# Score products with k's low part and the sample's value products on 128 rows instead of 64, in a two-layer attention and FFN trunk

## The chip, the cores and the metric

One Trainium2 chip, one of its cores. The metric is the device time of one execution in microseconds (us), median of the runs shown. Engines: PE is TensorE (matrix products; PEld its weight loads), DVE is VectorE, ACT ScalarE, POOL GpSimd, SP issues most DMAs.

## What is computed

Two layers of a streaming encoder, for a prompt of 512 tokens and a sample of 64 new tokens behind a cache of 128, with the same weights. Cut to what matters here:

```python
p = xn @ w_in                      # q k v of three branches A, B, C (8, 8, 4x2 heads of 64), gate logits
# A: band attention with a bias by distance; prompt and sample
logits = einsum('bqhd,bkhd->bhqk', q, keys) * 64**-0.5 + bias
o_a = einsum('bhqk,bkhd->bqhd', softmax(logits), vals)
# B: stick-breaking: weights from log_sigmoid(z) and reversed sums over keys of log_sigmoid(-z)
# C: two softmax maps per head, p0 - lam * p1, times v (128 wide), normalised per head
x = x + (sum_n sigmoid(gate_n) * (o_n @ w_branch[n])) @ w_out
x = x + (gelu(causal_conv3(xn @ w_gate)) * (xn @ w_up)) @ w_down
```

All in float32.

## The kernel before

**Tokens and weights.** The 64 sample tokens and the 512 prompt tokens stand side by side as 576 columns, worked in two halves of 288. The weights come in chunks of 512 KB. Each product of the main stream is split: a value is written as a high part (fp32r) and a low part (the rest), and hi\*hi, hi\*lo and lo\*hi are summed in PSUM. So a chunk of eight 128-row blocks is 48 products of 288 columns, named `mv..`, `mk..`, `mq..`, `mg..`, `mb..`, `mo`, `mu..`, `md` (the digit in a name is the layer, the last letter the branch, f the FFN; `mm` at L129 to L131 makes them all).

**Attention units.** A unit is 128 columns of q, k and v, that is two heads of 64. There are four units to a branch and layer, 24 in all. `prep_k` (L605) makes from k the tile KD: for head e, rows 64e to 64e+63 hold k's high part, and the other 64 rows a copy of k itself. `prep_q` (L634) makes X: q's high part on the same rows as k's high part, q's low part on the others. So one product of 128 rows gives hi\*hi + lo\*k. What is left, q's high part with k's low part, needs 64 rows: `prep_k` writes k's low part to KL on rows 64e to 64e+63, and `scores` (L656) and `zmm` in `head_b` (L881) issue behind each KD product a KL product over these 64 rows, into the same PSUM columns. The widths are 512, 384, 256 and 128 columns for a head (a causal triangle of tiles), so there are 4 KL products to a head.

**The sample.** Its attention weights come to `sw`: 128 cache keys in columns 0 to 127, the 64 new keys in columns 128 to 255 on 64 rows. `sample_pv` (L804) makes two products, cache values `cv` on 128 rows and new values `natsv` on 64 rows, in float32, for which the profile shows two records each.

**What sets the order.** Every engine works its own queue in order. The order is written out at build time: the main stream issues its products, and after each the generators of the attention steps are asked (`tick`, L141) whether their next step is due by an estimate of the engines' clocks. The estimate of a product (L130) goes by its columns alone, not by its rows. Steps therefore stand between main products in fixed places, and an engine waits at its queue's head where a result is late.

**Buffers that the change touches.** KL (one buffer), `sw` (one), `natsv` (two, alternating), and `ch`, high parts of B's running sums (two buffers of their own). `bias` is a pair of 128x512 buffers, used in branches A and C only.

Of the kernel before, what the change touches and what calls it, by code (L numbers as in the profile page):

```python
# [16 lines left out]
P = 128  # L17
D = 1024
ND = 8
S = 512  # L20
# [13 lines left out]
# column blocks of P kept as keys by queries: (key tile -> offset in the 1280 wide layout)  # L34
SEG = {0: 0, 1: 512, 3: 896, 2: 1024}
# row blocks of P kept as queries by keys: (query tile -> offset in the 1280 wide layout)
# [9 lines left out]
def trunk_kernel(ctx: ExitStack, tc: tile.TileContext, a: dict, o: dict):  # L46
# [26 lines left out]
    # The order of issue follows an estimate of the engines' clocks: a generator's next step is  # L73
    # issued when what it depends on should be there, so that no engine waits at its queue's head.
    clk = {"PE": 0.0, "ACT": 0.0, "DVE": 0.0, "POOL": 0.0}
    cx = {"t": 0.0, "eng": None, "last": 0.0}
    gens = []  # [label, generator, time from which the next step may be issued]
# [100 lines left out]
    def bank(kind, nm, hold):  # L178
        """a PSUM bank, as soon as one is free in emission order; hold collects it for give()"""
        yield from until(lambda: free[kind] and min(free[kind]) <= clk["PE"])  # L180
        take(kind, nm, hold)
# [22 lines left out]
    # parameter rows -> per-partition columns  # L204
# [49 lines left out]
    stc = const.tile([P, 4, NF], F32, name="stc")  # L254
    identb = const.tile([P, P], BF16, name="identb")
# [5 lines left out]
    # every vector on 128 rows, so that a row pitch shorter by one reads shifted windows  # L261
# [22 lines left out]
    def bias_band(l, aid, tab, queue=nc.gpsimd):  # L284
        """bias by distance, one row per head: the reversed table of the band"""
        h = []
        yield from bank("z", f"ep{l}", h)
        ep = h[0][1]
        mm(ep[0:8, 0:P], tab[:, 1, :], aid, True, True)
        mm(ep[0:8, P:2 * P], tab[:, 0, :], aid, True, True)  # L290
        ev = slot(f"ev{l}")
        vector.memset(ev[0:8, 0:319], 0.0)
        vector.memset(ev[0:8, 575:576], 0.0)
        vector.tensor_copy(ev[0:8, 319:575], ep[0:8, 0:256])
        give(h)
        vector.tensor_scalar(ev[0:8, 0:319], ev[0:8, 0:319], ev[0:8, 319:320], None, op0=ALU.add)
        queue.dma_start(ebias[l * 8:l * 8 + 8, :], ev[0:8, 0:EW])

    def bias_buckets(t5t, oh):
        """the same of the shared buckets"""  # L300
        ev = slot("ev5")
        for c0, cn in ((0, 512), (512, 64)):
            h = []
            yield from bank("z", f"ep5{c0}", h)
            ep = h[0][1]
            mm(ep[0:4, 0:cn], t5t, oh[0:32, c0:c0 + cn], True, True)
            vector.tensor_copy(ev[0:4, c0:c0 + cn], ep[0:4, 0:cn])
            give(h)
        nc.gpsimd.dma_start(ebias[16:20, :], ev[0:4, 0:EW])

    def setup(aid, tabs, t5t, oh):
        """constants of the later steps, between the first chunks"""
# [10 lines left out]
        for l in range(DEPTH):  # L323
            nb = const.tile([P, 24], F32, name=f"nbg{l}")
            vector.tensor_scalar(nb, par[l, 0][:, 16:40], -1.0, None, op0=ALU.mult)
            par[l, 2] = nb
            lam_init = 0.8 - 0.6 * math.exp(-0.3 * l)
            ls = const.tile([P, 2], F32, name=f"ls{l}")
            lt = sm.tile([P, 64], F32, tag="lt", name=f"lt{l}", bufs=1)
            for j in range(2):  # L330
                vector.tensor_tensor_reduce(out=lt, in0=lp[:, l, 2 * j, :], in1=lp[:, l, 2 * j + 1, :], scale=1.0,
                                            scalar=0.0, op0=ALU.mult, op1=ALU.add, accum_out=ls[:, j:j + 1])
            yield
            scalar.activation(ls, ls, AF.Exp)
            yield
            nl = const.tile([P, 1], F32, name=f"nlam{l}")
            # -(e0 - e1 + init) = (e1 - init) - e0
            vector.scalar_tensor_tensor(nl, in0=ls[:, 1:2], scalar=-lam_init, in1=ls[:, 0:1],
                                        op0=ALU.add, op1=ALU.subtract)
            lamc[l] = nl  # L340
            sc = const.tile([P, 1], F32, name=f"sub{l}")
            vector.tensor_scalar(sc, par[l, 0][:, 40:41], 1.0 - lam_init, None, op0=ALU.mult)
            subc[l] = sc
# [12 lines left out]
    chunks = []  # L356

    def chunk(nm, src, kt, act, evac, ncol=1, pre=None, pre_ev=None, post=None, norm=None, half=None, twin=None):
        """half: only one half of the tokens; twin: the earlier chunk whose weights serve again"""
# [15 lines left out]
    def split(i):  # L375
        """the weights' high and low parts, half a chunk at a time"""
# [91 lines left out]
    # Newton's step for r = rsqrt(v) from a = K rsqrt(v), K^3 = 1/2:  r = (3 K^2 - v a^2) a  # L468
    KR = 0.5 ** (1.0 / 3.0)

    def rstd_steps(ps, n, r, t):
        """r = rsqrt(mean + eps) of a PSUM region; exp/ln with a Newton step; t scratch"""
# [24 lines left out]
    def norm_tile(nm, d, x, g):  # L497
        """x * g split for the products, squares summed"""
# [46 lines left out]
    def load_bias(row, nm):  # L545
        """[queries, 512 keys], right aligned; the last 64 keys are hidden from the first 64 queries"""
# [13 lines left out]
    def natural(u, src, off, kind):  # L560
        """[cols, tokens] -> token rows: the k / v outputs, and v for P V"""
# [15 lines left out]
        nats = sm.tile([T, P], F32, tag="nats" + kind, name=f"nats{kind}{nm}", bufs=2 if kind == "v" else 1)  # L577
# [8 lines left out]
    def prep_v(u):  # L586
# [4 lines left out]
        u["vns"] = u["nats"]  # L591
# [14 lines left out]
    def prep_k(u):  # L606
# [4 lines left out]
        KL = ap_.tile([P, S], F32R, tag="KL", name=f"KL{nm}", bufs=1)  # L611
        u["KD"], u["KL"] = KD, KL
# [7 lines left out]
        for e in range(2):  # L620
# [8 lines left out]
            vector.tensor_tensor(KL[r, :], kp[r, :], KD[r, e, :].bitcast(F32), op=ALU.subtract)  # L629
# [26 lines left out]
    def scores(u, e, qt, z, c0):  # L656
        n = (qt + 1) * P
        r = slice(64 * e, 64 * e + 64)
# [3 lines left out]
        mm(out, u["X"][r, e, qs], u["KL"][r, 0:n], False, True)  # L662
        return out

    def soft(u, e, A, st, b, qts, nm, after):
        """exp(logits - max) of some query tiles, laid out by query, and 1 / sum"""
# [21 lines left out]
    def to_keys(A, nm, ph, pl, grp, flag):  # L688
        """[q, keys] -> [keys, q], hi and lo"""
# [22 lines left out]
    def pv_head(u, e, ph, pl, dst, nm):  # L712
        """dst[64e:64e+64, T:] = (P V)^T of head e"""
# [60 lines left out]
    def sample_soft(u, nm, b):  # L774
# [24 lines left out]
        w = sm.tile([P, 256], F32, tag="sw", name=f"sw{nm}", bufs=1)  # L799
# [6 lines left out]
    def sample_pv(u, w, nm, h):  # L806
# [4 lines left out]
        mm(ps[:, 0:P], u["vns"], w[0:64, P:2 * P], False, True)  # L811
# [16 lines left out]
    def softplus_to(dst, z):  # L828
        """dst = max(z, 0) + ln(1 + exp(-|z|))"""
# [7 lines left out]
    def sample_b(u):  # L837
# [4 lines left out]
        # both heads side by side, keys of the cache | new keys (rows past 64 masked)  # L842
# [10 lines left out]
        w = sm.tile([P, 256], F32, tag="sw", name=f"sw{nm}", bufs=1)  # L853
# [6 lines left out]
    def head_b(u, e):  # L860
        l, br, p, nm0 = u["id"]
        nm = f"{nm0}{e}"
        X, KD, KL = u["X"], u["KD"], u["KL"]
        r = slice(64 * e, 64 * e + 64)
        A = wide("a", f"A{nm}")
        sh, sl = wide("ph", f"sh{nm}", F32R), wide("pl", f"sl{nm}", F32R)
        ch = ap_.tile([P, 384], F32R, tag="ch", name=f"ch{nm}", bufs=2)
# [4 lines left out]
        def zmm(z, kt, c0, start):  # L872
# [4 lines left out]
            mm(out, KL[r, ks], X[r, e, kt * P:512], False, False)  # L877
# [8 lines left out]
        def keep(sg, z, flag):  # L886
            """softplus of z, in two parts"""
# [5 lines left out]
        def weights(sg, z, hold, flag, eng):  # L893
            """exp of the finished exponents, in two parts"""
# [22 lines left out]
        # sums over later key tiles, kept by query: kt 2 += kt 3  # L917
# [5 lines left out]
        # kt 1 += kt 2  # L923
# [18 lines left out]
        for t_, c_ in ((sh, ch), (sl, cl)):  # L942
            mm(z0, negt, t_[:, g0], False, False)
            mm(z0[:, P:512], negones, c_, False, t_ is sl)
        yield
# [5 lines left out]
    def head_c(u):  # L951
# [48 lines left out]
        # headwise norm over the 128 values (partitions)  # L1000
# [37 lines left out]
    def spawn_attention(u):  # L1038
# [7 lines left out]
        else:  # L1046
            u["left"], u["qk"] = 3, 9 if br == 0 else 3
# [8 lines left out]
    def unit(l, br, p, prev, prev2, first):  # L1056
# [5 lines left out]
        # while slots are free, v and q needn't share one place  # L1062
# [27 lines left out]
        def pre_q():  # L1090
# [6 lines left out]
            elif br == 2:  # L1097
                u["bias"] = [load_bias(16 + p, nm)]
# [14 lines left out]
    def sigmoid_steps(g, l, br, c):  # L1113
        # sigmoid(y) = exp(-ln(1 + exp(-y)))
# [43 lines left out]
    def layer(l):  # L1158
# [38 lines left out]
        # w_out and the residual  # L1197
# [22 lines left out]
        # FFN  # L1220
# [94 lines left out]
        def down_final(fs):  # L1315
            """one half of the tokens after the other, so that the first half's rows leave meanwhile"""
# [41 lines left out]
        # the states of the last f are there before the last group of w_down starts  # L1358
# [11 lines left out]
    fin = {"n": [0, 0], "ys": []}  # L1370
    # rows of each half: first column, rows, where they go
# [30 lines left out]
    def final_rstd(h, rp):  # L1402
        """1 / rms of the rows of a half, one column pair per block of rows"""
# [46 lines left out]
    def final_second():  # L1450
        """rows of the second half as their tiles get ready; they stay in PSUM"""
# [35 lines left out]
    def load_x(i):  # L1487
        """all prompt rows of a quarter of the columns"""
# [31 lines left out]
    # the first three chunks grow with the rows of x as they get turned  # L1520
# [46 lines left out]
    def split_first(i):  # L1567
        """chunks 0 and 1 in slots, as three are held at a time"""
# [101 lines left out]
def _constants():  # L1670
# [3 lines left out]
    # keys (rows) by queries (columns): masked where key >= query; sample: two heads of 64 queries  # L1674
# [31 lines left out]
```

## Time and profile before

| | |
|---|---|
| median of three runs | 2258.51 us (2256.84 to 2266.4) |
| profiled execution, first to last instruction | 2255.2 us |
| PE busy | 2230.0 us (99%), 15911 products |
| DVE / ACT / POOL busy | 1395.3 (62%) / 1044.5 (46%) / 397.2 (18%) us |
| DMA | 200.5 MB, mean 89 GB/s |
| mean granted TensorE clock | 0.988 of full speed |

How to read it: the span is divided nearly wholly among products on PE, so what counts is how far each product's start lies from the next one's. A product's own "busy" time includes its way through the array and overlaps the next; the distance of starts doesn't. Two forms appear in a row: `128*128 128x288` says rows\*columns of the weights that stand in the array, then rows x columns of what is streamed through it. The trunk's attention lies at about 45 to 640 us (layer 0) and 1155 to 1700 us (layer 1), the FFN behind each.

### The profile page before, as it was taken

Reading aid. Unit: us, or ns where it says so; the run is one execution under the profiler, and the core shown is the slowest. Engines: PE = TensorE matmul, PEld = TensorE weight load, DVE = VectorE, ACT = ScalarE, POOL = GpSimd, SP = SyncE. Lnnn points to the kernel's source line nnn. Section 1 sums busy time; section 2 is a strip of 40 time slices with the busy share of each in tenths; the row PEclk is TensorE's granted clock in tenths of the full one; section 3 lists DMA queues with packets and bytes.
Section 4 is the critical chain, followed back from the end, with each engine's and each line's share of the span. In section 5 each row is a group of like instructions: output and inputs, shape, how many; then the busy total and the mean of one; then the engine's idle time right before and its main releaser. Section 6 shows DMA issues by size and latency. Waiting matters only on the chain.

```text
span 2255.2 us, 39749 instructions
## 1 busy us (share of the span) xinstructions
PE 2230.0 (99%) x15911; PEld 2136.7 (95%) x15911; DVE 1395.3 (62%) x2852; ACT 1044.5 (46%) x2057; POOL 397.2 (18%) x520
## 2 busy tenths in 40 slices
PE   8999999999999999999999999999999999999998
PEld 7989999999999999999998999999999999999998
DVE  7786655666556656556567656566674666556564
ACT  5557666544534323223345477665445343223334
POOL 2012121111032212112110111211110222112121
PEclk9999999999999999999999999999999999999999
DMA  7342222222232222222242322222222423222222
GB/s 212 96 137 75 84 73 77 76 87 74 80 123 75 85 85 85 84 83 79 92 134 72 101 58 78 74 76 85 76 88 80 126 66 95 84 85 85 75 85 72
DMA packets 326563, 200.50 MB, mean 89 GB/s; under 512 B 10544, under 2 KB 320754, under 8 KB 326314
## 3 DMA queue, kind: packets, MB, share of 16 engines
q1 hardware_dynamic: 324618, 194.88, 29.0%
q0 software_dynamic: 1760, 3.08, 0.4%
q8 instruction: 125, 2.05, 0.4%
q14 instruction: 60, 0.49, 0.1%
HBM read 176.54 MB, written 25.83 MB: 90 GB/s over the span
## 4 chain that ended last, share of the span: by engine, by line
PE 93%; DVE 4%; issue 1%; ACT 1%; POOL 1%; DMA 0%; SPq 0%; DVEq 0%; POOLq 0%; ACTq 0%
PE md L131 11%; PE mg1f L131 6%; PE mg0f L131 6%; PE mu1f L131 6%; PE mu0f L131 6%; PE mo L131 4%; PE mg0b L131 3%; PE mg1b L131 2%; PE mg1a L131 2%; PE mg0a L131 2%; PE mg0c L131 2%; PE mg1c L131 2%; PE mv1a L131 1%; PE mv1b L131 1%; PE mk1a L131 1%; PE mb0a L131 1%
## 5 line engine op out<-in xcount | busy, mean ns | idle before, releaser
L102 DVE TENSOR_TENSOR x<-md,x 128x288 f32<-128x288 f32 x192 | 86.7, 454 | 117.1 <-PE md L131 116.3
L102 ACT CAST whid<-wrd 128x512 fp32r<-128x512 f32 (+1 forms) x88 | 46.8, 579 | 138.0 <-PE md L131 87.9
L131 PE MATMUL md<-hh0f,whid 128*128 128x288 f32 x352 | 104.9, 298 | 3.5 <-DVE x L102 3.5
L131 PE MATMUL mu0f<-xhf,wlou0f 128*128 128x288 f32 x352 | 103.8, 295 | 0.0
L131 PE MATMUL mu1f<-xhf,wlou1f 128*128 128x288 f32 x352 | 103.8, 295 | 0.0
L131 PE MATMUL md<-hh0f,wlod 128*128 128x288 f32 x352 | 103.8, 295 | 0.0
L131 PE MATMUL mg0f<-xhf,whig0f 128*128 128x288 f32 x352 | 103.8, 295 | 0.0
L131 PE MATMUL mg1f<-xhf,whig1f 128*128 128x288 f32 x352 | 103.8, 295 | 0.0
L131 PE MATMUL mg0f<-xhf,wlog0f 128*128 128x288 f32 x352 | 103.7, 295 | 0.0
L131 PE MATMUL mg1f<-xhf,wlog1f 128*128 128x288 f32 x352 | 103.7, 295 | 0.0
L131 PE MATMUL mu0f<-xlf,whiu0f 128*128 128x288 f32 x352 | 103.7, 295 | 0.0
L131 PE MATMUL mu1f<-xlf,whiu1f 128*128 128x288 f32 x352 | 103.7, 295 | 0.0
L131 PE MATMUL md<-hl0f,whid 128*128 128x288 f32 x352 | 103.6, 294 | 0.0
L131 PE MATMUL mg0f<-xlf,whig0f 128*128 128x288 f32 x352 | 103.6, 294 | 0.0
L131 PE MATMUL mg1f<-xlf,whig1f 128*128 128x288 f32 x352 | 103.6, 294 | 0.0
L131 PE MATMUL mu0f<-xhf,whiu0f 128*128 128x288 f32 x352 | 103.6, 294 | 0.0
L131 PE MATMUL mu1f<-xhf,whiu1f 128*128 128x288 f32 x352 | 103.6, 294 | 0.0
L131 PE MATMUL md<-hh1f,whid 128*128 128x288 f32 x288 | 85.7, 297 | 2.7 <-DVE x L102 2.7
L131 PE MATMUL md<-hh1f,wlod 128*128 128x288 f32 x288 | 84.9, 295 | 0.0
L131 PE MATMUL md<-hl1f,whid 128*128 128x288 f32 x288 | 84.8, 294 | 0.0
L131 PE MATMUL mo<-ml,whio 128*128 128x288 f32 x256 | 75.6, 295 | 0.8 <-DVE ml L102 0.8
L131 PE MATMUL mo<-mh,wloo 128*128 128x288 f32 x256 | 75.5, 295 | 0.0
(957 smaller groups left out, 8519.4 us busy)
## 6 DMA issues: line engine op xcount, KB each, us to landing
wrd<-in_w_down SPq DMA_DIRECT2D x40, 512.0 KB
wrg0f<-in_w_up SPq DMA_DIRECT2D x22, 512.0 KB
wru0f<-in_w_up SPq DMA_DIRECT2D x22, 512.0 KB
wrg1f<-in_w_up SPq DMA_DIRECT2D x22, 512.0 KB
wru1f<-in_w_up SPq DMA_DIRECT2D x22, 512.0 KB
wro<-in_w_out SPq DMA_DIRECT2D x16, 512.0 KB
xspill<-x SPq DMA_DIRECT2D x16, 288.0 KB
x<-xspill SPq DMA_DIRECT2D x16, 288.0 KB
```

Source lines behind the costliest of these rows:

```text
L102: return f(*args, **kw)
L131: nc.tensor.matmul(out, lhsT=lhsT, rhs=rhs, start=start, stop=stop, skip_group_check=True)
```

## The change

KL becomes one constant tile with a plane for each head. Its other 64 rows are set to zero once at the start, `prep_k` writes k's low part on the 64 rows as before, and the KL products run over all 128 rows of X and KL: the zero rows add nothing. `sw` and the two `natsv` buffers become constant tiles too; their rows 64 to 127 are zero from the start (in branch B, `sw` is written whole each time by an exponential of masked values), and the second sample product runs over 128 rows. To make room, B's `ch` tiles take the `bias` buffers, idle in B, and the q chunk of the first two C units waits in the written order until the last B unit's `ch` products are issued.

```diff
+    KL = const.tile([P, 2, S], F32R, name="KL")
+    natsv = [const.tile([P, P], F32, name=f"natsv{i}") for i in range(2)]
+    sw = const.tile([P, 2 * P], F32, name="sw")
+    for i in range(4):
+        cs = slice(i * P, (i + 1) * P)
+        vector.tensor_scalar(KL[64:128, 0, cs], onesd[64:128, :], 0.0, None, op0=ALU.mult)
+        vector.tensor_scalar(KL[0:64, 1, cs], onesd[0:64, :], 0.0, None, op0=ALU.mult)
+    for t in (*natsv, sw[:, P:2 * P]):
+        gpsimd.memset(t[64:128, :], 0.0)
 ...
-            vector.tensor_tensor(KL[r, :], kp[r, :], KD[r, e, :].bitcast(F32), op=ALU.subtract)
+            vector.tensor_tensor(KL[r, e, :], kp[r, :], KD[r, e, :].bitcast(F32), op=ALU.subtract)
 ...
-        mm(out, u["X"][r, e, qs], u["KL"][r, 0:n], False, True)
+        mm(out, u["X"][:, e, qs], KL[:, e, 0:n], False, True)
 ...
-        mm(ps[:, 0:P], u["vns"], w[0:64, P:2 * P], False, True)
+        mm(ps[:, 0:P], u["vns"], w[:, P:2 * P], False, True)
 ...
-        ch = ap_.tile([P, 384], F32R, tag="ch", name=f"ch{nm}", bufs=2)
+        ch = ap_.tile([P, 512], F32R, tag="bias", name=f"ch{nm}", bufs=2)[:, 0:384]
 ...
-            mm(out, KL[r, ks], X[r, e, kt * P:512], False, False)
+            mm(out, KL[:, e, ks], X[:, e, kt * P:512], False, False)
 ...
+                drain_while(lambda: prev is not None and prev.get("ch", 2 if prev["id"][1] == 1 else 0) > 0, "ch")
```

On PE, ACT and SP the built instructions stand in the same order before and after, one for one. DVE and POOL get instructions at the start alone. DVE's queue before, from its first instruction of the kernel (`ones`, `epsc` are constants, `g` the gains of the first norm, `xst` the sample's rows):

```order
L102 MEMSET onesd 128x128
L102 TENSOR_SCALAR ones_88<-onesd 128x128
L102 MEMSET epsc 128x1 x2
L102 COPY g_152<-g_150 128x8
L102 COPY xst<-xts 128x512
```

and now:

```order
L102 MEMSET onesd 128x128
L102 TENSOR_SCALAR ones_88<-onesd 128x128
L102 MEMSET epsc 128x1 x2
L102 TENSOR_SCALAR KL<-onesd 64x128 x8
L102 COPY g_167<-g_165 128x8
L102 COPY xst<-xts 128x512
```

Eight instructions that write KL's zeros stand ahead of the copy of `g`; POOL gets three memsets of 64x128 ahead of its first DMA. At run time a few instructions wait for more than before: the first `ch` cast of each layer for old bias loads, and the first bias load and memset of a C unit for the `ch` products of the last B unit.

## Rows read from the trace of the kernel before

**Rows 1.** The page: busy time by engine; the chain that ended last.

```profile
PE 2230.0 (99%) x15911; PEld 2136.7 (95%) x15911; DVE 1395.3 (62%) x2852; ACT 1044.5 (46%) x2057; POOL 397.2 (18%) x520
...
PE 93%; DVE 4%; issue 1%; ACT 1%; POOL 1%; DMA 0%; SPq 0%; DVEq 0%; POOLq 0%; ACTq 0%
```

**Rows 2.** Waits of PE, 45 to 1690 us: total us, times, longest us.

```profile
PE md L131 <- DVE x L102: 3.5, 9, 0.7
```

**Rows 3.** Timeline, PE and PEld: start, duration, engine, line, operation, form [idle before].

```profile
46.02 0.19 PEld L131 LDWEIGHTS mk0a<-xhm,whik0a 128*128 128x128 f32 x1
46.15 0.29 PE L131 MATMUL mk0a<-xhm,whik0a 128*128 128x288 f32 x1
...
49.96 0.18 PEld L131 LDWEIGHTS s0a<-KL0a,X0a 64*128 64x128 f32 x1 [0.19 <-issue]
49.96 0.44 PE L131 MATMUL s0a<-KL0a,X0a 64*128 64x384 f32 x1
```

**Rows 4.** Timeline of PE: scores of the first C unit, twelve products up to 395.30.

```profile
391.07 0.40 PE L131 MATMUL s0c<-KD0c,X0c 128*128 128x512 f32 x1
391.40 0.50 PE L131 MATMUL s0c<-KL0c,X0c 64*128 64x512 f32 x1
...
395.30 0.40 PE L131 MATMUL mb0a<-oh0a,whib0a 128*128 128x288 f32 x1
```

**Rows 5.** Timeline of PE: products on 128 rows without a KL product near.

```profile
358.60 0.28 PE L131 MATMUL zb0b<-ch0b,tri 128*128 128x256 f32 x1
358.72 0.34 PE L131 MATMUL zb0b<-sl0b,tri 128*128 128x384 f32 x1
...
369.50 0.40 PE L131 MATMUL zc0b<-sh0b,tri 128*128 128x512 f32 x1
369.73 0.33 PE L131 MATMUL zc0b<-ch0b,tri 128*128 128x384 f32 x1
369.91 0.39 PE L131 MATMUL zc0b<-sl0b,tri 128*128 128x512 f32 x1
...
376.50 0.22 PE L131 MATMUL o0b<-sh0b,VS0b 128*128 128x128 f32 x1
376.56 0.22 PE L131 MATMUL o0b<-sl0b,VS0b 128*64 128x128 f32 x1
```

**Rows 6.** Timeline of PE: scores of a B head, nine products up to 1296.10.

```profile
1294.25 0.22 PE L131 MATMUL za1b<-X1b,KD1b 128*128 128x128 f32 x1
...
1294.65 0.23 PE L131 MATMUL za1b<-mbs,identb 128*128 128x128 bf16 x1
1294.69 0.36 PE L131 MATMUL za1b<-X1b,KD1b 128*128 128x256 f32 x1
...
1296.10 0.31 PE L131 MATMUL za1b<-X1b,KD1b 128*128 128x128 f32 x1
```

**Rows 7.** KL's products in layer 0's branch A: count, duration ns min/median/max, first and last start.

```profile
L131 PE MATMUL s0a<-KL0a,X0a x32: 322/439/686, 49.2 to 154.3; 64*128 64x512 f32 x8, 64*128 64x384 f32 x8, 64*128 64x256 f32 x8, 64*128 64x128 f32 x8
```

**Rows 8.** Timeline of PE: the sample's value products of one unit.

```profile
1239.75 0.48 PE L131 MATMUL spv1a<-sw1a,natsv1a 64*128 64x128 f32 x2
1240.17 0.40 PE L131 MATMUL mk1a<-xhm,whik1a 128*128 128x288 f32 x1
```

**Rows 9.** The ten stretches at half clock ahead of 2250 us, by engine: their sum.

```profile
sum 51.20, PE 51.20 PEld 46.91 DVE 34.01 ACT 31.10 POOL 3.22; mean PE 5.12 PEld 4.69 DVE 3.40 ACT 3.11 POOL 0.32
```

**Rows 10.** Timeline of PE inside one of these stretches.

```profile
1232.20 0.44 PE L131 MATMUL mv1a<-xhm,whiv1a 128*128 128x288 f32 x1
1232.44 0.44 PE L131 MATMUL mv1a<-xlm,whiv1a 128*128 128x288 f32 x1
```

**Rows 11.** Branch A of layer 0: us, busy time of PE, PEld, DVE, ACT, POOL; clock.

```profile
45.00:175.00 130.00, 130.00 (x833) 114.25 (x833) 101.22 (x292) 68.31 (x164) 16.82 (x32) 0.95 0.39 112
```

**Rows 12.** Timeline of DVE at the start; issue of the first C bias on SP's queue.

```profile
3.12 0.17 DVE L102 COPY g<-g 128x8 f32<-128x8 f32 x1 [1.85 <-PE g L135]
...
375.39 0.53 SPq L548 DMA_DIRECT2D bias0c<-ebias  x1
```

More of the change, by code (lines that the diff above doesn't have):

```diff
@@ L576, in natural @@
         yield
-        nats = sm.tile([T, P], F32, tag="nats" + kind, name=f"nats{kind}{nm}", bufs=2 if kind == "v" else 1)
+        if kind == "v":
+            nats = natsv[(br * 4 + p) % 2][0:T, :]
+        else:
+            nats = sm.tile([T, P], F32, tag="natsk", name=f"natsk{nm}", bufs=1)
         vector.tensor_copy(nats, tp2[0:T, 0:P])
@@ L590, in prep_v @@
         yield from natural(u, u["vf"], 0, "v")
-        u["vns"] = u["nats"]
+        u["vns"] = natsv[(br * 4 + p) % 2]
         vn = u["nat"]
@@ L610, in prep_k @@
         KD = ap_.tile([P, 2, S], F32R, tag="KD", name=f"KD{nm}", bufs=1)
-        KL = ap_.tile([P, S], F32R, tag="KL", name=f"KL{nm}", bufs=1)
-        u["KD"], u["KL"] = KD, KL
+        u["KD"] = KD
         h = []
@@ L657, in scores @@
         n = (qt + 1) * P
-        r = slice(64 * e, 64 * e + 64)
         qs = slice(qt * P, qt * P + P)
@@ L798, in sample_soft @@
         yield
-        w = sm.tile([P, 256], F32, tag="sw", name=f"sw{nm}", bufs=1)
+        w = sw
         vector.tensor_copy(w[:, 0:P], tp[:, 0:P])
@@ L852, in sample_b @@
         yield
-        w = sm.tile([P, 256], F32, tag="sw", name=f"sw{nm}", bufs=1)
+        w = sw
         scalar.activation(w, z[:, 0:256], AF.Exp)
@@ L862, in head_b @@
         nm = f"{nm0}{e}"
-        X, KD, KL = u["X"], u["KD"], u["KL"]
-        r = slice(64 * e, 64 * e + 64)
+        X, KD = u["X"], u["KD"]
         A = wide("a", f"A{nm}")
         sh, sl = wide("ph", f"sh{nm}", F32R), wide("pl", f"sl{nm}", F32R)
-        ch = ap_.tile([P, 384], F32R, tag="ch", name=f"ch{nm}", bufs=2)
+        ch = ap_.tile([P, 512], F32R, tag="bias", name=f"ch{nm}", bufs=2)[:, 0:384]
         cl = ap_.tile([P, 384], F32R, tag="cl", name=f"cl{nm}", bufs=2)
@@ L944, in head_b @@
             mm(z0[:, P:512], negones, c_, False, t_ is sl)
+        u["ch"] -= 1
         yield
@@ L1046, in spawn_attention @@
         else:
-            u["left"], u["qk"] = 3, 9 if br == 0 else 3
+            u["left"], u["qk"], u["ch"] = 3, 9 if br == 0 else 3, 2 if br == 1 else 0
             spawn(lab, (head_a if br == 0 else head_b)(u, 0))
```

## Prediction

> **What bounds the kernel now.** The page comes first: PE is busy 99% of the span and makes up 93% of the chain that ended last [rows 1]. The waits of PE say the same from the other side: over the whole stretch that holds attention, its largest wait for another engine adds up to 3.5 us [rows 2]. So what shortens PE's own sequence shortens the kernel, until another engine becomes late. Busy time doesn't tell whether PE's time is well spent, so the next view is the timeline, and there the distance from one start to the next. A main product of 288 columns takes 0.13 us, and its weights are loaded while the product ahead of it still runs: the load at 46.02 is 0.13 us ahead of its product [rows 3]. At a KL product this isn't so. Load and product start together at 49.96, and the load follows 0.19 us in which PEld stood idle [rows 3]. The idle time is put down to nothing else that the profile shows ("issue"). A load takes about 0.18 us [rows 3], so a product whose load isn't hidden should cost that much more, and the KD product behind it the same on the way back.
>
> **What a pair costs now, and what on 128 rows.** The first C unit's score run has six pairs (KD and KL of 512, 512, 384, 384, 256 and 128 columns); from 391.07 to 395.30 they take 4.23 us [rows 4]. The price of products that stay on 128 rows: 0.23 us at 512 columns, 0.18 at 384, 0.12 at 256, 0.06 at 128 [rows 5]. These rows also hold accumulation into one PSUM region and new weights at every product, as the pairs have them, and one product on 64 columns of weights, which follows at 0.06 us like the rest: fewer columns cost nothing, so what costs at KL is rows. The six pairs at these prices are 2 x (2 x 0.23 + 2 x 0.18 + 0.12 + 0.06) = 2.00 us. The run gives back 4.23 - 2.00 = 2.23 us, or 0.37 a pair. Both ways at 0.19 would be 0.38, so the two readings agree. A B head has three pairs and three masks in 1296.10 - 1294.25 = 1.85 us, a mask taking 0.04 [rows 6]. At full price that is 2 x (0.06 + 0.12 + 0.18) + 0.12 = 0.84 us, so 1.01 / 3 = 0.34 a pair. Each branch has 32 KL products in a layer, as the row of A's shows [rows 7], so A and C have 128 in the two layers and B 64: 128 x 0.37 + 64 x 0.34 = **69 us**.
>
> **The sample.** The trace before has no float32 value product of new keys on 128 rows. Its two records on 64 rows take 1240.17 - 1239.75 = 0.42 us [rows 8]. The nearest rows bound the gain: nothing, if the doubled work of float32 is what costs, and 0.4 if it pays entry, middle and exit. I take 0.3, near the pair's 0.37, since it too leaves 128 rows and returns. 24 units make 24 x 0.3 = **7 us** (bounds 0 to 10).
>
> **The clock.** The granted clock stands at half (1.2 instead of 2.4 GHz) in ten stretches ahead of the last microseconds, 51.2 us in all [rows 9]. Ahead of every one of the ten PE had been in a run of score pairs; it never fell in the FFN, which is denser. At half clock a main product takes 0.24 us [rows 10] instead of 0.13 [rows 3]. So these stretches hold 51.2 x (1 - 0.13 / 0.24) = 23 us that full clock would give back. The pairs above were priced in runs at full clock, so nothing is counted twice. If runs of half the length leave PE without its gaps, the falls should go. But in branch A a new wait may stand right behind a run (below), so I take two thirds, **16 us** (bounds 0 and 23).
>
> **What becomes late.** PE's and DVE's queues keep their order, and PE now reaches the steps that read DVE's results sooner. In branch A of layer 0 DVE works 101 of 130 us [rows 11]. PE would give up 32 x 0.37 + 4 x 0.3 = 13 us there, and half of what its lower clock (0.95) costs, some 3 us: 114 us, of which DVE fills 89%. Two in-order queues that wait for each other in turn don't run that full, so part is lost to waits of PE for the sample's softmax and for v's evacuation on DVE. No row prices this wait; it lies between zero and all that an A unit gains, 13 / 4 + 1 = 4 us, eight units, 32 us. I take 1.5 us a unit, **12 us** back, nearer to zero because DVE itself waits for PE's scores now and moves up with them. Its upper end in the range is 3 us a unit, 24. Branches B and C are priced at none: C's DVE stands idle through a score run, and B's pairs are spread between main products.
>
> **Edits at nothing.** The eight zeroing instructions lie in the 1.85 us in which DVE waits at its start for PE [rows 12]; if they outlast it, the excess delays the copy of `g` by a fraction of a microsecond, once. POOL's three memsets are small beside the time until its tables are used. The new wait on SP: the first C bias load was issued at 375.39 [rows 12], and the last B unit's `ch` product that frees its buffer started at 369.73 [rows 5], 5.7 us sooner. Both move together; were it the other head's, the weight chunks queued behind on SP would be late by about a microsecond, twice in the kernel. ACT's `ch` casts wait for bias loads long landed. KL, `sw` and `natsv` have as many buffers as before, and `prep_k` writes the same rows.
>
> **Sum.** 69 + 7 + 16 - 12 = 80 us off the profiled span: 2255 - 80 = 2175. The median of the runs is 2258.5, 3.3 us above that span; so **2178 us** (0.964 of before).
>
> **Rivals.** *DVE takes over* (0.08): the waits eat the clock's gain and most of A's. 76 - 32 - 10 = 34 us remain: 2225 us. For it speaks DVE's share in branch A; against it that DVE's waits for scores shrink too.
>
> *The loads stay exposed* (0.05): what makes the load late isn't the change of rows but something that KD and KL share, and 128 rows don't mend it. Then the sequence keeps its gaps and the time is 2258 us. Against it stand the rows of B's sums, which load new weights for each product and accumulate likewise at full rate [rows 5]. The Trainium skill has a rule for this rival: in "TensorE: Matmul & The Clock Gate", section "Part 3: Packing small matmuls — row/col tiling", a weight load overlaps running products only where the row groups differ. By that rule loads for 128 rows behind 128 rows would never be hidden. The trace disagrees: main products load ahead on the same 128 rows [rows 3].
>
> *Slower by the clock* (0.03): PE arrives at the steps behind each score run before DVE is through, stands there, and the clock falls behind every run, not behind ten. A fall of the mean length of now, 5.1 us [rows 9], costs 5.1 x 0.46 = 2.3 us. The kernel has 48 such runs (one in a unit of A, three in B, two in C), so up to 48 x 2.3 = 110 us instead of 23. With 76 gained and 24 lost in waits it would be 110 - 23 - 52 = 35 us slower: 2294 us. It decides against the change from (23 + 52) / 2.3, some 33 such falls, on. The ten falls of now, in runs that have gaps at every product, speak against it.
>
> *More than the sum* (0.04): nothing waits, all falls go, and the sample gives 10 us: 69 + 10 + 23 = 102 us, 2156 us.
>
> **How the numbers follow.** The forecast has the remaining 0.80. Its own bounds: 69 + 7 + 23 - 0 = 99 us, that is 2159, and 69 + 7 + 0 - 24 = 52 us, that is 2206. The range 2158 to 2208 leaves out the rivals, 0.20 in all. What a measurement of this kernel can tell from no change is about 0.5%, 11 us. Faster by more: forecast, more than the sum, DVE takes over, 0.92; within it: exposed loads, 0.05; slower: 0.03.
>
> **What would show it.** Right: the KL products appear as 128\*128, start 0.06 to 0.23 us before their followers, and their loads start ahead of them; the first C unit's twelve products take 2.0 us; fewer than four stretches at half clock; PE shows new waits for DVE in branch A of about 12 us in all, hardly any in B and C. Wrong: distances near 0.4 us at KL products (the rows weren't the cause), or a wait for DVE or a `bias` load of 30 us and more.

## The result, and the profile after

The changed kernel takes **2164.82 us** (median; 2164.67 to 2165.1) against 2260.91 for the kernel before beside it: a ratio of 0.958, interval 0.9561 to 0.9598. The forecast was 2178 in a range of 2158 to 2208. The profiled spans are 2255.2 and 2163.0 us, so 92.2 us are to be found; the forecast had 80. One execution of `dbl128` among the experiments below, the one that was profiled, had a granted clock of 0.65 from its first microseconds to its end and took 2993.78 us, for a reason that no run here shows, so the time of `dbl128` below is the median of the other three.

The page after, lines that answer [rows 1]:

```profile
PE 2135.8 (99%) x15911; PEld 2099.8 (97%) x15911; DVE 1393.0 (64%) x2860; ACT 1041.3 (48%) x2057; POOL 398.1 (18%) x523
...
PE 92%; DVE 5%; issue 1%; ACT 1%; POOL 1%; DMA 0%; SPq 0%; DVEq 0%; POOLq 0%; ACTq 0%
```

PE has the same 15911 products, is still busy 99% and still holds the chain. Nothing has taken over; its sequence got shorter.

The timeline of PE and PEld in the first unit of branch A, answering [rows 3]:

```profile
49.33 0.19 PEld L131 LDWEIGHTS s0a<-KD0a,X0a 128*128 128x128 f32 x1
49.55 0.34 PE L131 MATMUL s0a<-KD0a,X0a 128*128 128x384 f32 x1
49.55 0.19 PEld L131 LDWEIGHTS s0a<-KL,X0a 128*128 128x128 f32 x1
49.73 0.34 PE L131 MATMUL s0a<-KL,X0a 128*128 128x384 f32 x1
```

In [rows 3] KL's load started with its product, at 49.96, behind 0.19 us of an idle PEld. Now it starts at 49.55, together with the product *ahead* of it, 0.18 us before its own product at 49.73, and the idle time is gone. The load of KD behind KL does the same on the way back (49.33, product at 49.55).

The first C unit's run, answering [rows 4]: twelve products.

```profile
363.56 0.39 PE L131 MATMUL s0c<-KD0c,X0c 128*128 128x512 f32 x1
363.79 0.39 PE L131 MATMUL s0c<-KL,X0c 128*128 128x512 f32 x1
...
365.49 0.27 PE L131 MATMUL s0c<-KL,X0c 128*128 128x128 f32 x1
365.60 0.35 PE L131 MATMUL mb0a<-oh0a,whib0a 128*128 128x288 f32 x1
```

From 363.56 to 365.60 they take 2.04 us instead of 4.23. A B head, answering [rows 6]:

```profile
1226.87 0.22 PE L131 MATMUL za1b<-X1b,KD1b 128*128 128x128 f32 x1
...
1227.05 0.20 PEld L131 LDWEIGHTS za1b<-X1b,KD1b 128*128 128x128 f32 x1
1227.09 0.36 PE L131 MATMUL za1b<-X1b,KD1b 128*128 128x256 f32 x1
1227.17 0.19 PEld L131 LDWEIGHTS za1b<-X1b,KL 128*128 128x128 f32 x1
1227.29 0.28 PE L131 MATMUL za1b<-X1b,KL 128*128 128x256 f32 x1
1227.41 0.23 PE L131 MATMUL za1b<-mbs,identb 128*128 128x128 bf16 x1
1227.45 0.42 PE L131 MATMUL zb1b<-X1b,KD1b 128*128 128x384 f32 x1
1227.71 0.33 PE L131 MATMUL zb1b<-X1b,KL 128*128 128x384 f32 x1
...
1227.92 0.31 PE L131 MATMUL za1b<-X1b,KD1b 128*128 128x128 f32 x1
```

Its nine products take 1.05 us, not 1.85; the forecast had 0.84 (the two PEld rows are read further below). The sample's value products, answering [rows 8]:

```profile
1207.55 0.39 PE L131 MATMUL spv1a<-sw,natsv 128*128 128x128 f32 x2
1207.69 0.38 PE L131 MATMUL mk1b<-xhm,whik1b 128*128 128x288 f32 x1
```

0.14 us to the next start, where it was 0.42. The waits of PE from 0 to 1690 us, answering [rows 2] (us in total, times, longest):

```profile
PE md L131 <- DVE x L102: 3.5, 9, 0.7
...
PE spt0a L135 <- DVE sA0a L102: 0.8, 1, 0.8
...
PE s0a L131 <- DVE KL L102: 0.7, 1, 0.7
```

The two lower ones, one instance each, are all that is new in attention. Branch A of layer 0, answering [rows 11], and the only stretch at half clock that is left (the columns are those of [rows 11]):

```profile
45.00:159.20 114.20, 112.66 (x835) 107.13 (x834) 99.01 (x293) 67.54 (x164) 18.07 (x31) 1.00 0.45 128
...
2157.59:2163.00 5.41, 0.00 (x0) 0.00 (x0) 0.92 (x2) 0.61 (x2) 0.00 (x0) 0.50 0.60 220
```

The product that started at 174.94 before starts at 159.18 now; the stretch took 130 us and takes 114.2. The clock stands at full where it stood at 0.95. The ten stretches of [rows 9] have all gone: what is left lies behind PE's last product.

**The account.** PE issues the same products in the same order in both traces, so each distance from one start to the next can be set against its partner. Distances at KL products at full clock gave back 17.9 us in A, 17.3 in B and 21.8 in C; those inside stretches at half clock, where price and clock are mixed, 7.1; those at the sample's value products 8.7; all other distances inside stretches at half clock 18.2; everything else 1.1. That makes 92.1.

### The profile page after: what moved, and what is told of

The parts are those of the page before. It is cut to its first block, busy times and chain, and to the rows that moved or that the text cites. A ratio compares the mean times of both kernels' runs of the same rounds, so it can differ in the third digit from the quotient of the medians.

```text
span 2163.0 us, 39766 instructions
## 1 busy us (share of the span) xinstructions
PE 2135.8 (99%) x15911; PEld 2099.8 (97%) x15911; DVE 1393.0 (64%) x2860; ACT 1041.3 (48%) x2057; POOL 398.1 (18%) x523
## 4 chain that ended last, share of the span: by engine, by line
PE 92%; DVE 5%; issue 1%; ACT 1%; POOL 1%; DMA 0%; SPq 0%; DVEq 0%; POOLq 0%; ACTq 0%
PE md L131 11%; PE mg1f L131 6%; PE mg0f L131 6%; PE mu0f L131 6%; PE mu1f L131 6%; PE mo L131 4%; PE mg0a L131 2%; PE mg1a L131 2%; PE mg0b L131 2%; PE mg1b L131 2%; PE mg0c L131 2%; PE mg1c L131 2%; DVE wlod L102 1%; PE mb1a L131 1%; PE mb0a L131 1%
## 5 line engine op out<-in xcount | busy, mean ns | idle before, releaser
L131 PE MATMUL md<-hh0f,whid 128*128 128x288 f32 x352 | 104.9, 298 | 3.5 <-DVE x L102 3.5
L131 PE MATMUL mu0f<-xhf,wlou0f 128*128 128x288 f32 x352 | 103.8, 295 | 0.0
L131 PE MATMUL mu1f<-xhf,wlou1f 128*128 128x288 f32 x352 | 103.8, 295 | 0.0
L131 PE MATMUL md<-hh0f,wlod 128*128 128x288 f32 x352 | 103.8, 295 | 0.0
L131 PE MATMUL mg1f<-xhf,whig1f 128*128 128x288 f32 x352 | 103.7, 295 | 0.0
L131 PE MATMUL mg0f<-xhf,whig0f 128*128 128x288 f32 x352 | 103.7, 295 | 0.0
L131 PE MATMUL mg0f<-xhf,wlog0f 128*128 128x288 f32 x352 | 103.7, 295 | 0.0
L131 PE MATMUL mg1f<-xhf,wlog1f 128*128 128x288 f32 x352 | 103.7, 295 | 0.0
L131 PE MATMUL mu1f<-xlf,whiu1f 128*128 128x288 f32 x352 | 103.7, 295 | 0.0
L131 PE MATMUL mu0f<-xlf,whiu0f 128*128 128x288 f32 x352 | 103.7, 295 | 0.0
L131 PE MATMUL mu0f<-xhf,whiu0f 128*128 128x288 f32 x352 | 103.6, 294 | 0.0
L131 PE MATMUL mu1f<-xhf,whiu1f 128*128 128x288 f32 x352 | 103.6, 294 | 0.0
L131 PE MATMUL md<-hl0f,whid 128*128 128x288 f32 x352 | 103.6, 294 | 0.0
L131 PE MATMUL mg0f<-xlf,whig0f 128*128 128x288 f32 x352 | 103.6, 294 | 0.0
L131 PE MATMUL mg1f<-xlf,whig1f 128*128 128x288 f32 x352 | 103.6, 294 | 0.0
L131 PE MATMUL md<-hh1f,whid 128*128 128x288 f32 x288 | 85.7, 297 | 2.7 <-DVE x L102 2.7
L131 PE MATMUL md<-hh1f,wlod 128*128 128x288 f32 x288 | 84.9, 295 | 0.0
L131 PE MATMUL md<-hl1f,whid 128*128 128x288 f32 x288 | 84.8, 294 | 0.0
L131 PE MATMUL mo<-ml,whio 128*128 128x288 f32 x256 | 75.6, 295 | 0.8 <-DVE ml L102 0.8
L131 PE MATMUL mo<-mh,wloo 128*128 128x288 f32 x256 | 75.5, 295 | 0.0
```

The source lines that it names most:

```text
L131: nc.tensor.matmul(out, lhsT=lhsT, rhs=rhs, start=start, stop=stop, skip_group_check=True)
```

## The experiments

**Theories.** Mine: a product on 64 rows between products on 128 rows can't have its load hidden, and neither can the product behind it, so PE pays at entry and exit of each visit to 64 rows (a visit: from 128 rows to 64 and back, however many products it holds). Rivals: every KL product has an exposed load of its own, whatever stands next to it; any change of the number of rows costs; the gain comes from the edits beside it (order, buffers, constant tiles) or from the clock alone. The single edits start from the changed kernel.

**Everything but the rows.** `rows64` puts both kinds back on 64 rows and leaves new tiles, zeros and waits as they are. `k_only` puts back the sample alone, `s_only` KL alone:

```diff
# rows64 and s_only (the like in head_b)
-        mm(out, u["X"][:, e, qs], KL[:, e, 0:n], False, True)
+        r = slice(64 * e, 64 * e + 64)
+        mm(out, u["X"][r, e, qs], KL[r, e, 0:n], False, True)
# rows64 and k_only
-        mm(ps[:, 0:P], u["vns"], w[:, P:2 * P], False, True)
+        mm(ps[:, 0:P], u["vns"][0:64, :], w[0:64, P:2 * P], False, True)
```

> The changed kernel with both kinds of products back on 64 rows; constant KL, sw and natsv tiles, the zeroing at the start, ch in the bias buffers and the extra waits stay. If the rows are the whole cause: the time of before, 2261 us within 5 us, ten or so stretches at half clock. If the buffers or waits had a part: clearly off, by the size of that part (2250 us and less if they helped, 2268 and more if they cost).

> Only the KL products on 128 rows, the sample's value products back on 64. In the traces of before and after the sample's intervals differ by 8.7 us, so 2165 + 9 = 2174 us, at full clock. If the sample's product is hidden beside something: 2165 us.

> Only the sample's value products on 128 rows, the KL products back on 64. Additive parts: 2261 - 9 = 2252 us, and the stretches at half clock stay, since they follow score runs. If the sample's gain was only there because the clock was full: 2256 us or more.

`rows64` took 2259.63 us, ratio 0.9995 (0.9974 to 1.0015): the edits beside it are nothing, for or against. `k_only` took 2173.84 (0.962; 0.9598 to 0.9642) with the clock at full throughout, 9.0 us above the changed kernel; `s_only` 2255.51 (0.998; 0.9962 to 0.9998). The account of `s_only`'s trace gives the sample 8.7 us, as in the changed kernel, and its stretches at half clock are still there. By its time `s_only` lies only 4.1 us below `rows64`, near the 2256 of its second expectation. The mean granted clock of its ten runs is 0.9837, against 0.9863 in the ten of `rows64`: some 12 us more at half clock, and at 46% of that lost some 5 us, about what is missing of the 8.7. Whether that lower clock comes with the edit or by chance isn't shown. So the two kinds add up in the distances, and in the times where the clock is full (`k_only`); KL holds nearly all, and the clock's part came with KL's.

**A alone.** `pad_a` keeps 128 rows in branch A and for the sample; B's and C's KL products go back to 64.

```diff
+        r = slice(64 * e, 64 * e + 64) if u["id"][1] == 2 else slice(0, P)
+        mm(out, u["X"][r, e, qs], KL[r, e, 0:n], False, True)
```

> Branch A's KL products and the sample's on 128 rows, B's and C's KL products on 64. If a fall of the clock comes from the score run just ahead of it: A's five falls go, B's and C's five stay; the time is 2261 - 9 (sample) - 24 (A's pairs) - 11 (A's share of the 18 us at half clock) = 2217 us. If the clock depends on attention as a whole: all falls stay, 2228 us, or all go, 2209 us.

2215.75 us, 0.9808 (0.9785 to 0.9831). Its stretches at half clock, first and last of seven, and their sum (columns as in [rows 11]):

```profile
167.30:170.71 3.41, 3.41 (x15) 2.71 (x15) 0.00 (x0) 1.01 (x3) 0.00 (x0) 0.50 0.07 16
...
1518.98:1525.80 6.82, 6.82 (x28) 6.58 (x28) 4.82 (x18) 3.60 (x9) 0.81 (x1) 0.50 0.01 2
sum 27.29, PE 27.29 PEld 25.55 DVE 12.48 ACT 14.94 POOL 3.22; mean PE 3.90 PEld 3.65 DVE 1.78 ACT 2.13 POOL 0.46
```

None of the seven lies in branch A, where five of [rows 9]'s ten lay (and six of the eleven of `rows64`): three are in B, four in C. Where the 64-row products went, the falls went; where they stayed, the falls stayed.

**Is it the change of rows, or 64?** `rows72` runs head 0's KL products over 72 rows, the last eight of them zero.

```diff
+        r = slice(0, 128 if e else 72)
+        mm(out, u["X"][r, e, qs], KL[r, e, 0:n], False, True)
```

> The changed kernel with head 0's KL products over 72 rows (k's low part and 8 zero rows), head 1's over 128. If the price belongs to products on 64 rows or fewer: 2165 us as with 128. If it belongs to any change of the row count: 96 KL products pay 0.33 us again and some falls of the clock return, 2165 + 32 + 0 to 9 = 2197 to 2206 us.

2165.17 us, 0.957 (0.9541 to 0.9598): the same as 128 rows. The first C unit's run:

```profile
363.38 0.40 PE L131 MATMUL s0c<-KD0c,X0c 128*128 128x512 f32 x1
363.62 0.40 PE L131 MATMUL s0c<-KL,X0c 72*128 72x512 f32 x1
363.85 0.40 PE L131 MATMUL s0c<-KD0c,X0c 128*128 128x512 f32 x1
```

0.23 to 0.24 us both ways. So my theory was too wide: changing from 128 rows to 72 costs nothing, changing to 64 does; numbers between were not run. A rule of the Trainium skill fits that. "TensorEngine Tiling (Array Packing)", "Tiling Modes", "Key Properties", says that a change of tiling mode (as against a change of tile) drains TensorE, and its list of modes goes from 128 rows to 64 to 32, so that 72 rows would share a mode with 128. By the list 64 columns would be a mode of their own too, and this case's trace shows no price there: the product on 128\*64 starts 0.06 us behind its neighbour, like one on 128\*128 [rows 5].

**Each load, or each visit?** `dbl64` issues every KL product of `rows64` twice in a row, `dbl128` every one of the changed kernel, so that the low part counts double in both. If every 64-row load is exposed, the second one pays as well; if entry and exit are what costs, it pays its columns only.

```diff
         mm(out, u["X"][r, e, qs], KL[r, e, 0:n], False, False)
+        nc.tensor.matmul(out, lhsT=u["X"][r, e, qs], rhs=KL[r, e, 0:n], start=False, stop=True, skip_group_check=True)
```

> KL products on 64 rows, each issued twice in a row (k's low part then counts twice; the second is extra work); the sample's too on 64 rows; order otherwise as it was. If only the change of rows costs: 192 x 0.15 us more than with single products, 2261 + 28 = 2289 us. If every load for 64 rows is exposed, change or not, by 0.1 us (as the sample's second record) 2308 us, by 0.2 us 2327 us. More falls of the clock may add some 10 us.

> The changed kernel with each KL product on 128 rows issued twice in a row (k's low part counts twice). The control for the other doubling: 192 x 0.15 us = 28 us, 2193 us, at full clock. If loads on 128 rows too lag behind in narrow products: up to 2200 us.

`dbl128` took 2193.95 us: 29.1 above the changed kernel, 0.15 a product. That is the bare price of the columns, a mean of (0.23 + 0.18 + 0.12 + 0.06) / 4 [rows 5]. `dbl64` took 2312.7 (1.0224; 1.0192 to 1.0257), 53 us above `rows64`. By the total that reads like a further 0.1 us of exposed load at each of the 192 products. The trace says otherwise. A C unit of `dbl64` (L131 is the first issue, L675 the second):

```profile
411.94 0.50 PE L131 MATMUL s0c<-KL,X0c 64*128 64x512 f32 x1
412.28 0.39 PE L675 MATMUL s0c<-KL,X0c 64*128 64x512 f32 x1
412.60 0.49 PE L131 MATMUL s0c<-KD0c,X0c 128*128 128x512 f32 x1
413.02 0.49 PE L131 MATMUL s0c<-KL,X0c 64*128 64x512 f32 x1
```

and PEld there (the bracket is its idle time ahead):

```profile
411.94 0.18 PEld L131 LDWEIGHTS s0c<-KL,X0c 64*128 64x128 f32 x1 [0.27 <-issue]
412.05 0.19 PEld L675 LDWEIGHTS s0c<-KL,X0c 64*128 64x128 f32 x1
412.60 0.19 PEld L131 LDWEIGHTS s0c<-KD0c,X0c 128*128 128x128 f32 x1 [0.37 <-issue]
```

The second 64-row load starts at 412.05, 0.23 us ahead of its product: it is hidden. Only the first one's and that of KD behind it start with their products. Beside it the same place in `rows64`:

```profile
395.19 0.49 PE L131 MATMUL s0c<-KL,X0c 64*128 64x512 f32 x1
395.61 0.50 PE L131 MATMUL s0c<-KD0c,X0c 128*128 128x512 f32 x1
396.04 0.50 PE L131 MATMUL s0c<-KL,X0c 64*128 64x512 f32 x1
```

One KL and its KD take 0.85 us there (395.19 to 396.04), 0.39 more than two products at 0.23; two KL and their KD take 1.08 (411.94 to 413.02), 0.39 more than three. The price is that of one visit, whatever is done in it. Over all widths the extra product costs about 0.16 us at full clock, some 30 us in all. The rest of the 53 is the clock. The sums over the stretches at half clock, `rows64` (eleven stretches), then `dbl64` (sixteen):

```profile
sum 54.61, PE 54.61 PEld 50.09 DVE 34.57 ACT 29.70 POOL 2.40; mean PE 4.96 PEld 4.55 DVE 3.14 ACT 2.70 POOL 0.22
```

```profile
sum 109.23, PE 109.23 PEld 92.38 DVE 46.65 ACT 55.42 POOL 2.40; mean PE 6.83 PEld 5.77 DVE 2.92 ACT 3.46 POOL 0.15
```

54.6 us more at half clock, of which 46% is lost, are 25 us; with the 30, that is 55 for the 53. That doubling the 64-row work doubles the time at half clock is measured; why is not settled here.

**Visits gathered.** `adj_c` stays on 64 rows, but in branch C the two heads' scores are issued together: their KD products first, then their KL products, head 0's on rows 0 to 63, head 1's on 64 to 127. A C unit then leaves 128 rows three times instead of eight. `adj_c128` is the same order on 128 rows. (In both, the narrower last pair of tiles shares a PSUM bank and the second start drops the first tile's KD sum; `adj_c128b` starts the bank once.)

```diff
+        for e in range(2):
+            for i, qt in enumerate(qts):
+                mm(zs[e][i], X[:, e, qt * P:qt * P + P], KD[:, e, 0:(qt + 1) * P], True, False)
+        for i, qt in enumerate(qts):
+            for e in range(2):
+                r = slice(64 * e, 64 * e + 64)   # adj_c; all 128 rows in adj_c128
+                mm(zs[e][i], X[r, e, qt * P:qt * P + P], KL[r, e, 0:(qt + 1) * P], False, True)
# adj_c128b: the KD product's True is i == 0
```

> Products on 64 rows as before the change, but in branch C the two heads' KD products come first, then their KL products next to each other, one head's on rows 0 to 63 and the other's on rows 64 to 127: three visits to 64 rows in a C unit instead of eight, all 64 KL products still there. If the price, 0.39 us, is one of the visit (in and out): 8 units x 5 x 0.39 = 16 us less than 2260, 2244 us, a few us less where falls of the clock go too. If every product on 64 rows pays for itself: 2260 us. If the two row halves run side by side: a further 5 us, 2239 us, and their starts lie 0.03 us or less apart.

> The changed kernel, all on 128 rows, with branch C's products in the same new order as in the kernel beside it. The control for the order: 2165 us, 2 or 3 us more where PSUM banks are held longer. Were it faster than the changed kernel, the order itself would be worth something.

`adj_c` took 2232.98 us, 0.988 (0.9848 to 0.9913), lower than expected. The first C unit, PE and PEld (x2 is both heads' product):

```profile
391.03 0.50 PE L131 MATMUL s0c<-KL,X0c 64*128 64x512 f32 x2
391.45 0.30 PEld L131 LDWEIGHTS s0c<-KD0c,X0c 128*128 128x128 f32 x2 [0.24 <-issue]
391.46 0.61 PE L131 MATMUL s0c<-KD0c,X0c 128*128 128x384 f32 x2
```

Two KL products of 512 columns fill 0.43 us (391.03 to 391.46), where one fills 0.42 in `rows64` (395.19 to 395.61): their starts lie 3 to 4 ns apart in the records, so the two row halves of the array work side by side. The Trainium skill says this in "TensorE: Matmul & The Clock Gate", "Part 3: Packing small matmuls — row/col tiling": products on different row groups run at once, some 4 ns apart; the trace agrees. All score products of C take 22.7 us, against 42.3 in `rows64` and 19.6 in the changed kernel. The 4.7 us of columns that side by side saves and 24 visits in place of 64 account for it at 0.33 us a visit: 19.6 - 4.7 + 24 x 0.33 = 22.8. With C's visits gathered, its falls of the clock went as well: four of `rows64`'s eleven lay in C, none of the nine that `adj_c` has ahead of its end does. But A and B have nine here instead of seven with nothing changed in them, so the time at half clock only went from 54.6 to 47.8 us, worth 3 us. (`adj_c128` and `adj_c128b` below take the same time, so the dropped sum has no part in `adj_c`'s.)

**Was DVE close behind?** `no_kl` leaves the KL products out of the changed kernel; their estimated time is still counted when the order is written, so what is left keeps its order.

> The changed kernel without the KL products (the term of q times k's low part is left out). It tells how much room DVE and ACT leave. If PE stays the bound: 192 x 0.15 = 28 us less, 2137 us, PE's waits in branch A under 5 us. If DVE is close behind PE in branch A, as the prediction took: A's third of the gain is lost in waits and more, 2147 to 2155 us.

2142.41 us, 22.4 below the changed kernel and between the two expectations. Their columns alone are 192 x 0.148 = 28 us, so some 6 us of that did not come. Its waits of PE, 45 to 1690 us:

```profile
PE spt0a L135 <- DVE sA0a L102: 2.0, 4, 0.8
PE ntk0a L135 <- DVE sst0a L102: 1.7, 1, 1.7
PE spt1a L135 <- DVE sA1a L102: 1.6, 4, 0.4
```

These three come to 5.3 us, where the changed kernel has 0.8. They are the waits for the sample's softmax that I feared for the change itself, and they come a step later: PE has to give up the KL products' columns as well before they show. The rest of the 6 us is the clock. One stretch at half clock came back:

```profile
54.49:57.90 3.41, 3.27 (x15) 3.24 (x16) 3.30 (x17) 3.41 (x13) 0.00 (x0) 0.50 0.22 64
```

It is worth 3.41 x 0.46 = 1.6 us, and with the 4.5 us of waits that makes 6.1. In the 7 us ahead of it PE has no product on 64 rows, but it has the wait of 1.7 us and one of 0.8. So a run of 64-row products isn't the only thing that a fall follows here: one came behind waits, as the prediction feared.

**The other order on 128 rows.** `adj_c128` took 2161.52 us (0.9564; 0.9528 to 0.96), 3.3 us below the changed kernel, so `adj_c128b` was measured beside the changed kernel itself:

> The changed kernel once more, to stand beside the next run on the same chip. Every theory expects 2165 us, ratio 0.957 to 0.958 against the kernel before. Where it differs from 2164.8 by more than 1 us, differences of a few microseconds between kernels of different calls can't be read.

> The changed kernel with the other order of C's score products (all KD products of both heads, then all KL products, all on 128 rows), now with each group's sum kept whole. If what costs at a KL product is only its 64 rows, the order of products on 128 rows is worth nothing by itself, and what is left is where the softmax steps behind them fall: 2161 to 2165 us. If the order without any change of rows were worth what adj_c gained (27 us), it would be near 2140; if the later first score of head 0 made PE wait, 2170 or more.

The changed kernel again: 2165.11 (2164.63 to 2165.4, five runs). `adj_c128b`: 2161.56 (2161.22 to 2162.07, four runs). The runs don't overlap; 3.5 us, 0.16%. C's products did not get faster: its KD products cost PE 1.0 us more in all, and the sample's scores in C (`ss0c`, `ss1c`) 0.7. What went is an old wait. PE from 45 to 2300 us in the changed kernel, a line that the kernel before has in the same words (`mb1b` has the same numbers in layer 1):

```profile
PE mb0b L131 <- DVE g0b L102: 1.2, 3, 0.4
```

Neither wait is among the waits of `adj_c128b`. The waits lie among C's units of q, k and v, where DVE reads B's gates out of PSUM (`g0b<-mb0b`). DVE in the changed kernel, then in `adj_c128b`:

```profile
408.51 0.46 DVE L102 TENSOR_TENSOR g0b<-mb0b,g0b 128x288 f32<-128x288 f32 x1
409.00 0.69 DVE L102 TENSOR_TENSOR X0c<-qf0c,X0c 64x512 fp32r<-64x512 f32 x1
409.72 0.46 DVE L102 TENSOR_TENSOR g0b<-mb0b,g0b 128x288 f32<-128x288 f32 x1
```

```profile
406.63 1.88 DVE L102 TENSOR_TENSOR X0c<-qf0c,X0c 64x512 fp32r<-64x512 f32 x2
408.54 0.46 DVE L102 TENSOR_TENSOR g0b<-mb0b,g0b 128x288 f32<-128x288 f32 x1
409.42 0.46 DVE L102 TENSOR_TENSOR g0b<-mb0b,g0b 128x288 f32<-128x288 f32 x1 [0.42 <-PE mb0b L131]
```

In the changed kernel a step that makes q's low part stands between two gate read-outs, and PE waits for the second one. In the other order both such steps stand ahead, and DVE waits for PE. Each of the six instances held a main product back by 0.55 us beyond its 0.13, 3.3 together; with smaller delays around them the distances at `mb0b` and `mb1b` shrank by 4.7. Less the 1.7 us that the others cost more, that is 3.0 of the 3.5. `adj_c` on 64 rows has lost these waits too, so 3.3 of its 27 us belong here and not to the visits.

## Why the prediction was right, point by point

**What bounds the kernel.** Right: PE's sequence, before and after.

**The pairs** (69 us). Right in cause, 5 us too large. At full clock a KL product gave back 0.33 us in A, 0.35 in C and 0.27 in B; with those at half clock it is 64.1 us. A and C fall short because narrow products don't reach full rate in a score run: the KL product of 128 columns takes 0.11 us to the next start (365.49 to 365.60), not 0.06, and in A the KD product of 512 behind it 0.28 (77.63 to 77.92), not 0.23. B was mis-sized by more, 17 us for 22: I priced the head at full rate throughout, but its KL product of 128 columns takes 0.12, and the KD product behind a mask (bf16, 0.04 us) takes 0.20 us to the next start at 256 columns (1227.09 to 1227.29) and 0.26 at 384 (1227.45 to 1227.71), not 0.12 and 0.18.

The load rows above show one cause for all of these. KD's load starts only with the mask, at 1227.05, and KL's 0.12 us behind it, at 1227.17. Over the changed kernel at full clock, of 14888 loads of 128 columns of weights by `mm` none is followed by the next one sooner than 0.108 us; behind loads of 64 columns the least is 0.055. A product of 0.04 or 0.06 us is over before the next load has had that time, so its follower is late by the rest: 0.12 - 0.04 = 0.08 behind a mask, 0.11 - 0.06 = 0.05 behind 128 columns. The mask's type isn't needed for it, since products of k and q show the same. The price of 0.06 was read from [rows 5] at 376.50, where the load to be hidden is one of 64 columns (`128*64`). The product behind the next full load, 256 columns at 376.62, takes 0.17 us there (to 376.79) and not 0.12; that row would have warned me. So in those rows the product with fewer columns of weights was not neutral: it saved half a load.

**The sample** (7 us, bounds 0 to 10). 8.7: two records on 128 rows cost 0.14 us, so the doubled work of float32 was no part of the old 0.42. 0.36 a unit, the same visit price as KL's.

**The clock** (16 of 23 us). 18.2 outside the KL distances, and a part of the 7.1 inside them. The falls went altogether; the third that I kept back for falls behind new waits wasn't needed here, though `no_kl` shows that such falls exist. `pad_a` and `adj_c` show that falls go where 64-row visits go.

**What becomes late** (12 us back, bounds 0 to 24). This is the term that was mis-sized: new waits came to 1.5 us in attention, no loss that the account can find (everything else gave +1.1). DVE works 99.0 of 114.2 us in branch A, 87%, about as I worked out, but two in-order queues stood that well: DVE's wait for PE's scores in branch A, 5.6 us before (`A0a` for `s0a`), is no longer among the waits listed, the least of which is 0.3, so DVE moved up with PE. That queues can't run that full was the step without a row, and it failed. `no_kl` shows how little room is left behind it.

**Edits at nothing.** Right: `rows64`. One detail, DVE at its start (answering [rows 12]):

```profile
1.28 2.20 DVE L102 TENSOR_SCALAR KL<-onesd 64x128 fp32r<-64x128 f32 x8
3.41 0.15 DVE L102 COPY g<-g 128x8 f32<-128x8 f32 x1
```

The zeroing takes 2.20 us, outlasts the 1.85 of idle, and the copy comes 0.29 late; at 45 us PE is 0.24 behind, once. The first C bias load still leaves SP behind the product that frees its buffer: issued at 348.45, the product started at 346.77.

**Sum.** Pairs -5, sample +2, clock +2, waits +12, the small rest +1: 80 becomes 92. The pairs' error hid part of the waits'. The step from span to median, taken as 3.3 us, is 1.8 after, another 1.5 of the 13 us between forecast and result.

**Rivals.** *Loads stay exposed*: fell, by the load rows above and by `rows64`. *DVE takes over* and *slower by the clock*: no sign (of the first one's sum, the last 10 us had no row behind them). *More than the sum* (2156) came closest in its mechanism, nearly nothing waiting and all falls gone, and in its time (2156 to the forecast's 2178); its pairs were 5 us too dear.

## What to carry to other kernels

A product over 64 rows between products over 128 costs 0.3 to 0.4 us beside its columns, once a visit: fill it up with zero rows (72 rows were enough here), or gather 64-row products on both row halves, side by side, in one visit. Look for it where a weight load starts with its product, and PEld's idle time ahead has no releaser but "issue". A total can mislead about such a price: `dbl64` had the total of the wrong theory, and only the trace parted the 30 us of products from the 25 of clock. And a price from a row holds with the loads that stand beside it: a product shorter than its follower's load costs that load's time.

## What the runs showed of the hardware that was not expected

- 72 rows run at the price of 128 (0.23 to 0.24 us at 512 columns), 64 at 0.43.
- A second 64-row product behind a first has its load hidden, 0.23 us ahead, so the price is at entry and exit of such a run.
- Twice the 64-row products raised the time at half clock from 54.6 to 109.2 us, though PE is never idle for more than 0.4 us in attention in either; with the visits gone (changed kernel), no stretch at half clock was left ahead of the last product, and in `no_kl` one came back behind a wait of 1.7 us.
- A load of 128 columns of weights is never followed by the next load in less than 0.108 us at full clock (14888 loads of the changed kernel), one of 64 columns in no less than 0.055; behind products of 0.04 and 0.06 us the follower is late by 0.08 and 0.05.
- Two products on the two row halves, back to back, start 3 to 4 ns apart (32 pairs in `adj_c`).
